# A hybrid attention, DeltaNet and ConvGLU layer: systems laid out in DRAM by DRAM to DRAM transfers, zeros stored at another place, and another distribution of late modulation

## The chip, the cores and the metric

The kernel runs on one core of a Trainium2 chip. The metric is the device time of one execution in microseconds. Three runs of the kernel before gave 1779.87, 1783.9 and 1786.72 us; their median is 1783.9 us. The core has a matrix engine (PE, with a separate weight load), three engines for elementwise work (DVE or VectorE, ACT or ScalarE, POOL or GpSimd) and SyncE (SP), which here only issues transfers. ACT issues some too. Sixteen DMA engines carry them.

## The reference, cut to what matters

The reference is one layer of a diffusion backbone, in float32, on 256 latent and 256 context tokens of width 2048. A normalised, modulated input goes through one wide projection; its columns feed latent attention (8 heads) and a gated DeltaNet (8 heads, two directions, chunks of 64 positions). Both branches are gated, added and projected; a gated MLP with a short convolution (ConvGLU) follows.

```python
shift1, scale1, gate1, shift2, scale2, gate2 = split(silu(c) @ w_ada + b_ada, 6)
p = modulate(rmsnorm(x, norm_mix), shift1, scale1) @ w_in    # and the same for ctx
# attention: 8 heads, latent queries over latent and context keys, one softmax
y_mla = softmax(q @ k.T / sqrt(192)) @ v
# DeltaNet, per head, direction and chunk of 64
m = where(strictly_lower, (beta * k) @ k.T * decay, 0)
u, w = triangular_solve(m + eye(64), [beta * v, beta * k * exp(gc)])
v_new = u - w @ s;  s = s * g_end + k_end.T @ v_new;  o = q @ s + A @ v_new
y_dn = rmsnorm(o) * silu(z)
x = x + gate1 * ((sig(g_a) * (y_mla @ w_o_mla) + sig(g_b) * (y_dn @ w_o_dn)) @ w_out)
x = x + gate2 * conv_glu(modulate(rmsnorm(x, norm_ffn), shift2, scale2))
```

The parts that the change touches are the 128 triangular systems of 64 x 64 (8 heads, 2 directions, 8 chunks) and the columns of `w_ada` that are needed late, for the second half of the layer.

## The kernel before

**Precision and the matrix work.** Every float32 product with a weight is split: ACT casts the weight to a high part (`whi`, L123), DVE computes the rest (`wlo`, L124), and PE multiplies with both (`mm_hl`, L156). Weights stream from DRAM in tiles of 512 KB (`raw`), issued by SP, with a ring of buffers. Each weight load waits until DVE and ACT have done with the buffer that it fills.

**Stages.** The first modulation and the first projections of all tokens come first (to about 145 us). Then the heads' stage builds, for each head, the inputs of the DeltaNet and the triangular matrices (to about 440 us). The attention follows in four pairs of heads (to about 722 us), then the scan of the DeltaNet, the output projections, and the ConvGLU (from about 1060 us, more than 700 us of matmuls).

**The systems.** The inverse of each 64 x 64 unit triangular matrix is built from 32 x 32 blocks. The two diagonal blocks of all 128 systems are read as one tile `ux` with 128 partitions and inverted on DVE by substitution (`inverse`, L822); `X[:, b]` is then the inverse of block b, one row of the tile for one system. `Xq` in DRAM takes it out of this form, once transposed (`xt`) and once as it stands; for groups of 16 systems q, `off_diagonal` (L855) reads it back as `xd` and multiplies it with the off-diagonal block `uo` on both sides, by PE with block diagonal tiles `bd`. All blocks end in the DRAM tensor `Tt`, which has for each direction and row of the 64 x 64 inverse 16 x 4 systems with 64 columns. The scan reads `Tt` from L1271 on (`tt<-Tt`, 721.7 us and later). The quarter of `Tt` below the diagonal is filled with zeros, by two transfers from the tile `none` (L656), issued by ACT at the start of the program.

**What sets the order.** Several generators are interleaved by hand: a `Side` runs its generator as far as a number of estimated nanoseconds that the main stream hands it. `fill` is the gate projections (L933), `inv` is `inverse` and then `off_diagonal`, `ada` the late modulation: 128 tiles of `wada2` (`rawa<-in_wada`, L262), each multiplied by a row and summed over its columns on DVE (1.2 us each). The attention's loop calls `side(c, r)` (L1179), which hands all three their share. PE's order is fixed where `pe.pinned` is set; `osync` and `odve` are the issuing engines with the place in the program kept, `sync`, `act` and `dve` can be shifted by the scheduler that lists each engine's instructions. `ada` must have reached fixed points before its sums are used, the last ones in the ConvGLU.

**Queues and counters.** Transfers issued by SP and by ACT signal their landing by eight counters, which the program uses in turn; an issuing engine works through its list in order, and a transfer that reuses a counter waits for the landing of the one before on it. In the listings below these counters are DMAHW0 to DMAHW7.

## Time and profile before

| What | Value |
| --- | --- |
| median of three runs | 1783.9 us (1779.87 to 1786.72) |
| the profiled execution's own time | 1786.89 us |
| its span (first to last instruction) | 1785.1 us |
| mean granted clock of PE | 0.985 |
| PE busy | 1737.5 us (97%) |
| DVE busy | 1356.8 us (76%) |
| ACT busy | 950.5 us (53%) |
| data moved by DMA | 417.15 MB in 190,260 packets, 56,912 of them under 512 B |

The profile is of one execution. Each row of a timeline gives the start in us, the duration, the engine, the line of the kernel, the operation and its tiles (output, arrow, input), and, in brackets, how long the engine stood idle before and what ended that. SPq and ACTq are the transfers' issues; an xN behind a row says that N like ones are put together, so the duration spans all of them with the pauses between. The table of windows has, for stretches of the span, the busy time and the number of instructions of each engine, the granted clock of PE (1.00 is full), the share of time in which the 16 DMA engines were busy, and the rate. The chain of waits follows the last instruction back to what released it.

The numbers of the stretches and of the waits are with the prediction.

### The profile page before, as it was taken

To read this page: it belongs to the slowest core of one execution; us is meant where nothing else is said; L and a number is where in the kernel's file an instruction comes from. 1 tells how busy PE (TensorE), PEld (TensorE's weight loads), DVE (VectorE), ACT (ScalarE), POOL (GpSimd) and SP (SyncE) were. 2 spreads that over 40 slices of the span, in tenths; PEclk is the share of its full clock that TensorE was granted. 3 is DMA by queue.
4 is the path that set the end of the run, shared out by engine and by line. 5 is a ranking of instruction groups with operands and counts; after the bars stand their busy time and mean duration, and the time that the engine had idled before them with its cause. 6 is when DMAs were issued, how large, how long until landed. Compare 5 with 4: busy or idle time off the path is not lost.

```text
span 1785.1 us, 34155 instructions
## 1 busy us (share of the span) xinstructions
PE 1737.5 (97%) x12957; PEld 1507.2 (84%) x12957; DVE 1356.8 (76%) x2696; ACT 950.5 (53%) x1966; POOL 41.4 (2%) x48
## 2 busy tenths in 40 slices
PE   7999999999799999999999999999999999999999
PEld 5887888888688888788878888888888888888888
DVE  4677799879578879787779979887788887655554
ACT  3335454454477766665646546555555555544443
POOL 0000011000000000000010000000000000000000
PEclk8999999999899999999989999999999999999999
DMA  9992588783578868999647968776667776666662
GB/s 348 407 373 93 150 235 249 230 257 109 138 255 248 260 214 273 360 339 361 233 130 233 328 199 281 232 237 207 202 219 229 228 225 201 182 198 199 198 199 87
DMA packets 190260, 417.15 MB, mean 234 GB/s; under 512 B 56912, under 2 KB 95696, under 8 KB 187792
## 3 DMA queue, kind: packets, MB, share of 16 engines
q1 hardware_dynamic: 165024, 401.59, 68.7%
q10 hardware_dynamic: 25072, 13.39, 2.5%
q8 instruction: 101, 1.65, 0.4%
q14 instruction: 63, 0.52, 0.1%
HBM read 387.00 MB, written 27.79 MB: 232 GB/s over the span
## 4 chain that ended last, share of the span: by engine, by line
PE 63%; issue 8%; DMA 1%; DVE 1%; ACT 0%; SPq 0%; POOL 0%; POOLq 0%; DVEq 0%
PE fps L68 27%; PE dps L68 13%; PE gtp L68 11%; PE brp L68 3%; PE vps L68 1%; PE kps L68 1%; PE qps L68 1%; PE sps L68 1%; PE kp L68 1%; PE ivp L68 1%; PE op L68 1%; PE yps L68 1%; PE yp L68 0%; DMA YM<-Ys 0%; SPq L851 0%
## 5 line engine op out<-in xcount | busy, mean ns | idle before, releaser
L123 ACT CAST whi<-raw 128x512 fp32r<-128x512 f32 (+1 forms) x940 | 578.9, 620 | 413.6 <-PE dps L68 113.5
L124 DVE TENSOR_TENSOR wlo<-raw,whi 128x512 fp32r<-128x512 f32 (+1 forms) x940 | 637.3, 686 | 211.4 <-ACT whi L123 203.5
L68 PE MATMUL fps<-H,whi 128*128 128x512 f32 x1376 | 475.0, 394 | 3.1 <-DVE H L1472 3.1
L68 PE MATMUL fps<-H,wlo 128*128 128x256 f32 x1376 | 372.3, 280 | 0.0
L68 PEld LDWEIGHTS fps<-H,whi 128*128 128x128 f32 x1376 | 253.7, 189 | 54.7 <-issue 1.9
L68 PEld LDWEIGHTS fps<-H,wlo 128*128 128x128 f32 x1376 | 259.7, 189 | 7.5 <-DVE wlo L124 0.5
L68 PE MATMUL gtp<-h,whi 128*128 128x512 f32 x640 | 231.4, 399 | 0.0
L68 PE MATMUL mmp<-h,whi 128*128 128x512 f32 x640 | 229.5, 400 | 0.0
L68 PE MATMUL dps<-GB,whi 128*128 128x512 f32 (+1 forms) x595 | 195.7, 377 | 0.0
L68 PE MATMUL mmp<-h,wlo 128*128 128x256 f32 x640 | 177.5, 283 | 0.0
L68 PE MATMUL gtp<-h,wlo 128*128 128x256 f32 x640 | 173.9, 282 | 0.0
L68 PE MATMUL dps<-GB,wlo 128*128 128x256 f32 x560 | 155.2, 282 | 0.0
L68 PEld LDWEIGHTS gtp<-h,whi 128*128 128x128 f32 x640 | 120.5, 190 | 25.3 <-issue 0.9
L68 PEld LDWEIGHTS mmp<-h,whi 128*128 128x128 f32 x640 | 119.8, 189 | 24.9 <-ACT dkx L531 0.3
L68 PEld LDWEIGHTS dps<-GB,whi 128*128 128x128 f32 x595 | 109.2, 188 | 20.2
L68 PEld LDWEIGHTS gtp<-h,wlo 128*128 128x128 f32 x640 | 121.5, 190 | 4.5
L68 PEld LDWEIGHTS mmp<-h,wlo 128*128 128x128 f32 x640 | 121.8, 190 | 3.6 <-issue 1.4
L68 PEld LDWEIGHTS dps<-GB,wlo 128*128 128x128 f32 x560 | 105.8, 189 | 0.6
L281 DVE CUSTOM_DVE_ANT_0 rawa<-rawa,sch 128x1024 f32<-128x1024 f32 x68 | 82.9, 1222 | 20.9 <-DMA rawa<-in_wada 19.4
L68 PE MATMUL fp<-h,gh 128*128 128x256 f32 (+1 forms) x448 | 85.5, 291 | 2.5 <-ACT h L68 1.7
L68 PEld LDWEIGHTS fp<-h,gh 128*128 128x128 f32 (+1 forms) x448 | 69.7, 190 | 7.6 <-issue 4.1
L68 DVE CUSTOM_DVE_ANT_0 rawa<-rawa,sch 128x1024 f32<-128x1024 f32 x60 | 72.9, 1218 | 0.0
(574 smaller groups left out, 2563.4 us busy)
## 6 DMA issues: line engine op xcount, KB each, us to landing
rawa<-in_wada SPq DMA_DIRECT2D x128, 512.0 KB, 5.2
raw<-in_wgate SPq DMA_DIRECT2D x82, 512.0 KB, 4.4
raw<-in_wval SPq DMA_DIRECT2D x82, 512.0 KB, 4.6
raw<-in_wdown SPq DMA_DIRECT2D x80, 512.0 KB, 4.2
wt<-in_wadas SPq DMA_DIRECT2D x16, 1024.0 KB, 9.6
raw<-in_wadab SPq DMA_DIRECT2D x32, 512.0 KB, 11.6
raw<-in_wgm SPq DMA_DIRECT2D x32, 512.0 KB, 5.6
raw<-in_wgd SPq DMA_DIRECT2D x32, 512.0 KB, 6.9
```

The lines of the kernel that those rows point to most:

```text
L68: i = f(*a, **k)
L123: act.copy(hi, raw)
L124: dve.tensor_tensor(out=lo, in0=raw, in1=hi, op=ALU.subtract)
L281: (odve if ada.bound else dve).tensor_tensor_reduce(out=w, in0=w, in1=sch, scale=1.0, scalar=0.0, op0=ALU.mult, op1=ALU.add, accum_out=par ...
```

## The change

It has five parts. (1) The two transfers of zeros to `Tt` are issued by SP, ahead of the heads' stage, and no longer by ACT at the start. (2) `inverse` stores three planes to `Xq` (the first block transposed, the first block, the second block), twelve transfers, and its sixteen stores `Tt<-ux` are gone. (3) A new function `place` copies blocks from DRAM to DRAM into `Tt`, for one q and one block in one transfer; `off_diagonal` calls it for the two diagonal blocks of each q, and for the off-diagonal one of the q before. (4) The off-diagonal block goes to a new DRAM tensor `Xo` by one transfer that ACT issues, where SP issued four to `Tt`. (5) `side` leaves `ada` out in the last four rounds of the attention's last pair and in the call behind it; those pieces of `ada` come later in the program.

```diff
--- before.py
+++ after.py
@@ -650,10 +650,9 @@
     Ud = dram.tile([4, 32, 2, 32, 32], F32, name="Ud")
     Uo = dram.tile([4, 32, 32, 32], F32, name="Uo")
 
-    Xq = dram.tile([2, 32, 4, 32, 32], F32, name="Xq")
+    Xq = dram.tile([3, 32, 4, 32, 32], F32, name="Xq")
+    Xo = dram.tile([32, 4, 32, 32], F32, name="Xo")
     Tt = dram.tile([P, 16, 4, 64], F32, name="Tt")
-    for d in range(2):
-        act.dma_start(Tt[64 * d + 32 : 64 * d + 64, :, :, 0:32].rearrange("c s g j -> c (s g) j"), none[:32].unsqueeze(1).broadcast_to([32, 64, 32]))
     As = dram.tile([4, P, 8, 64], F32, name="As")
     conv = mid.tile([P, 24, 3], F32, name="conv")
     dve.tensor_scalar(out=conv, in0=off["dn_conv"].rearrange("p (f w) -> p f w", w=3), scalar1=0.5, scalar2=None, op0=ALU.mult)
@@ -787,6 +786,8 @@
         gather(ps, P, xq[:, 0])
         return xs[0], xs[1], xq
 
+    for d in range(2):
+        osync.dma_start(Tt[64 * d + 32 : 64 * d + 64, :, :, 0:32].rearrange("c s g j -> c (s g) j"), none[:32].unsqueeze(1).broadcast_to([32, 64, 32]))
     ada = Side(ada_rest())
     ada.done, ada.bound = 0, True
     ins = {h: head_inputs(h) for h in (3, 0)}
@@ -842,13 +843,8 @@
         act.copy(xt, X[:, 0].rearrange("p c j -> p j c"))
         for g in range(4):
             gs = slice(32 * g, 32 * g + 32)
-            for n, x in enumerate((xt, X[:, 1])):
+            for n, x in enumerate((xt, X[:, 0], X[:, 1])):
                 sync.dma_start(Xq[n, :, g], x[gs])
-        for g in range(4):
-            for d in range(2):
-                for b in range(2):
-                    rs = slice(64 * d + 32 * b, 64 * d + 32 * b + 32)
-                    sync.dma_start(Tt[rs, :, g, 32 * b : 32 * b + 32].rearrange("c s j -> s c j"), X[32 * g + 16 * d : 32 * g + 16 * d + 16, b])
         yield 1000
         pI.close()
 
@@ -866,8 +862,13 @@
             sync.dma_start(uo, Uo[:, :, rs].rearrange("g j r i -> (g j) r i"))
             xd = pi.tile([P, 2, 4, 32], F32, tag="xd", name="xd", bufs=2)
             for n in range(2):
-                sync.dma_start(xd[:, n], Xq[n, rs].rearrange("r g j c -> (g j) r c"))
+                sync.dma_start(xd[:, n], Xq[2 * n, rs].rearrange("r g j c -> (g j) r c"))
             return uo, xd
+
+        def place(q, b, c, src):
+            rows = slice(64 * (q // 4) + 32 * b, 64 * (q // 4) + 32 * b + 32)
+            dst = Tt[rows, 4 * (q % 4) : 4 * (q % 4) + 4, :, 32 * c : 32 * c + 32]
+            sync.dma_start(dst.rearrange("c s g j -> (s g) c j"), src[4 * q : 4 * q + 4].rearrange("s g c j -> (s g) c j"))
 
         ahead = load(0)
         yield OD
@@ -875,6 +876,10 @@
             uo, xd = ahead
             if q < 7:
                 ahead = load(q + 1)
+            for n in range(2):
+                place(q, n, n, Xq[1 + n])
+            if q:
+                place(q - 1, 0, 1, Xo)
             for n in range(2):
                 src = uo if n == 0 else ip
                 for g in range(4):
@@ -887,10 +892,9 @@
                 if n == 0:
                     yield OC / 2
             act.copy(uo, ip)
-            for g in range(4):
-                dst = Tt[64 * (q // 4) : 64 * (q // 4) + 32, 4 * (q % 4) : 4 * (q % 4) + 4, g, 32:64]
-                sync.dma_start(dst, uo[32 * g : 32 * g + 32])
+            act.dma_start(Xo[4 * q : 4 * q + 4].rearrange("r g c i -> (g c) r i"), uo)
             yield OC / 2
+        place(7, 0, 1, Xo)
         pI.close()
 
     Ys = dram.tile([P, HEADS, T], F32, name="Ys")
@@ -1176,10 +1180,11 @@
     pairs = {}
     ryx = mid.tile([P, 2, T], F32, tag="krd", name="ryx")
 
-    def side(c, r):
+    def side(c, r, late=False):
         fill(r * c)
         inv(r * c)
-        ada(AD * c)
+        if not late:
+            ada(AD * c)
 
     pe.pinned = True
     for c in mla_project(0):
@@ -1206,10 +1211,10 @@
             for st in (pr, tail, at):
                 c = next(st, None)
                 if c is not None:
-                    side(c, R1 if b < 3 else 2.0)
+                    side(c, R1 if b < 3 else 2.0, b == 3 and n > 3)
             next(back, None)
         tail = at
-    side(2600, 1.0)
+    side(2600, 1.0, True)
     for _ in tail:
         pass
     inv.finish()
```

In the listings each engine's instructions stand in program order, with the counters or engines that an instruction waits for in brackets; names ending in q, s or a capital are tensors in DRAM or tiles as told above.

**SP at the start of the program** (`xl` and `xc` are the latent and the context tokens, `wt` the first weights). Before:

```order
L68 DMA xl<-in_xT 128x1024 [waits DMAHW0_49]
L68 DMA xc<-in_ctxT 128x1024 [waits DMAHW1_49]
L68 DMA xl<-in_xT 128x1024 [waits DMAHW2_49]
L68 DMA xc<-in_ctxT 128x1024 [waits DMAHW4_49]
L68 DMA wt<-in_wadas 128x2048 [waits DMAHW5_49]
L68 DMA wt<-in_wadas 128x2048 [waits DMAHW6_49]
```

and now:

```order
L68 DMA xl<-in_xT 128x1024
L68 DMA xc<-in_ctxT 128x1024 [waits DMAHW0_49]
L68 DMA xl<-in_xT 128x1024 [waits DMAHW1_49]
L68 DMA xc<-in_ctxT 128x1024 [waits DMAHW2_49]
L68 DMA wt<-in_wadas 128x2048 [waits DMAHW3_49]
L68 DMA wt<-in_wadas 128x2048 [waits DMAHW4_49]
```

The ninth load, the last `xc`, waited for the counter DMAHW4; it now waits for DMAHW2, and the others for counters one or two lower in the turn, since ACT's two transfers no longer take part here.

**SP at the end of the inverse** (`Xq`, `xd` and `Tt` as above; `raw<-in_wz` is the next weight of the gates). Before, behind the eight stores to `Xq` and fourteen of the sixteen to `Tt`:

```order
L851 DMA Tt<-ux 16x32x32 [waits DMAHW0_49]
L851 DMA Tt<-ux 16x32x32 [waits DMAHW1_49]
L869 DMA xd<-Xq 128x4x32 [waits DMAHW2_49]
L869 DMA xd<-Xq 128x4x32 [waits DMAHW3_49]
L869 DMA xd<-Xq 128x4x32 [waits DMAHW4_49]
L869 DMA xd<-Xq 128x4x32 [waits DMAHW5_49]
L129 DMA raw<-in_wz 128x1024 [waits DMAHW6_49,DVE_49]
L262 DMA rawa<-in_wada 128x1024 [waits DMAHW7_49,DVE_49]
L129 DMA raw<-in_wqb 128x1024 [waits DMAHW0_49,DVE_49]
```

and now, behind ten of the twelve stores to `Xq`:

```order
L847 DMA Xq<-ux 32x1024 [waits DMAHW4_49]
L847 DMA Xq<-ux 32x1024 [waits DMAHW5_49]
L865 DMA xd<-Xq 128x4x32 [waits DMAHW7_49,DMAHW6_49,DMAHW2_49]
L865 DMA xd<-Xq 128x4x32
L871 DMA Tt<-Xq 16x32x32 [waits DMAHW4_49,DMAHW0_49]
L865 DMA xd<-Xq 128x4x32 [waits DMAHW5_49,DMAHW1_49]
L865 DMA xd<-Xq 128x4x32
L871 DMA Tt<-Xq 16x32x32 [waits DMAHW3_49]
L129 DMA raw<-in_wz 128x1024 [waits DVE_49]
L262 DMA rawa<-in_wada 128x1024 [waits DVE_49]
```

The stores `Tt<-ux` are gone from ahead of the reads `xd<-Xq`; transfers `Tt<-Xq` stand between the reads, and the weights behind them. On DVE, the first instruction that makes use of the space that `ux` leaves is `km`, a key scale of the attention. Before:

```order
L124 TENSOR_TENSOR wlo<-raw,whi 128x512 [waits Activation_49]
L930 SCALAR_TENSOR_TENSOR zx<-zt,zx 128x256 [waits Activation_49]
L1035 SCALAR_TENSOR_TENSOR km<-ks,krm 128x4 [waits DMAHW4_49,DMAHW3_49,DMAHW5_49,DMAHW2_49,DMAHW6_49,DMAHW1_49,DMAHW7_49,DMAHW0_49,PE_49]
L124 TENSOR_TENSOR kt<-kps,kt 128x512 [waits Activation_49]
L1003 CAST rb_h<-km 128x4 [waits Pool_49]
```

and now:

```order
L124 TENSOR_TENSOR wlo<-raw,whi 128x512 [waits Activation_49]
L934 SCALAR_TENSOR_TENSOR zx<-zt,zx 128x256 [waits Activation_49]
L1039 SCALAR_TENSOR_TENSOR km<-ks,krm 128x4 [waits DMAHW4_49,DMAHW2_49,DMAHW5_49,DMAHW1_49,DMAHW6_49,DMAHW0_49,PE_49]
L124 TENSOR_TENSOR kt<-kps,kt 128x512 [waits Activation_49]
L1007 CAST rb_h<-km 128x4 [waits Pool_49]
```

It waited for all eight counters and now waits for six.

**ACT in the attention's last pair** (`s_` is a tile of scores: the exponential, then its normalisation; `ptp` and `PT` its transpose for PE; `YM` the attention's output, read back from `Ys` and split). Before:

```order
L1134 ACTIVATE s__8537,mns<-s__8537,mns,qm 128x512 [waits DVE_49]
L906 ACTIVATE zx<-zx 128x256 [waits DVE_49]
L123 CAST whi<-raw 128x512
L910 DMA Gs<-zx 128x256 [waits DMAHW3_49,Activation_49]
L1136 ACTIVATE s__8537<-s__8537,mns 128x512 [waits DVE_49]
L123 CAST PT<-ptp 128x4x128 [waits PE_49]
L123 CAST YM<-YM 128x2x256 [waits DMAHW1_49]
L123 CAST YM<-YM 128x2x256
```

and now:

```order
L1138 ACTIVATE s__8526,mns<-s__8526,mns,qm 128x512 [waits DVE_49]
L910 ACTIVATE zx<-zx 128x256 [waits DVE_49]
L123 CAST PT<-ptp 128x4x128 [waits PE_49]
L914 DMA Gs<-zx 128x256 [waits DMAHW7_49,Activation_49]
L123 CAST YM<-YM 128x2x256 [waits DMAHW5_49]
L1140 ACTIVATE s__8526<-s__8526,mns 128x512 [waits DVE_49]
L123 CAST YM<-YM 128x2x256
L123 CAST whi<-raw 128x512 [waits DMAHW1_49]
```

The first cast of `YM` stood behind the normalisation of the second tile of scores, and the transposes' cast `PT`; it now stands ahead of that normalisation.

## The prediction

> **What bounds the kernel now.** I read the page's first two parts, then the windows, then SP's timeline with the rows of PE, DVE and ACT beside it.
>
> ```profile
> span 1785.1 us, 34155 instructions
> PE 1737.5 (97%) x12957; PEld 1507.2 (84%) x12957; DVE 1356.8 (76%) x2696; ACT 950.5 (53%) x1966; POOL 41.4 (2%) x48
> ```
>
> PE is the bound: 1785.1 − 1737.5 = 47.6 us of idle time is all that waits can give back, beside the time lost to a reduced clock after them. PE's instructions and their order are the same in both kernels, so the change can only move waits. The windows show which resource is near its limit where the change works (columns: stretch, length, busy time and count of each engine, granted clock, DMA share, GB/s):
>
> ```profile
> 1.70:15.60 13.90, 10.15 (x72) 7.67 (x72) 7.24 (x15) 6.16 (x8) 0.20 (x2) 1.00 1.03 313
> 20.00:100.00 80.00, 74.01 (x840) 60.32 (x844) 50.16 (x75) 27.57 (x60) 1.02 (x1) 0.91 1.02 410
> 160.00:170.00 10.00, 10.00 (x39) 5.44 (x38) 7.76 (x13) 6.80 (x13) 0.00 (x0) 0.94 0.00 0
> 461.00:478.00 17.00, 11.21 (x87) 9.45 (x85) 4.22 (x7) 6.08 (x12) 0.00 (x0) 0.82 0.50 71
> 500.00:640.00 140.00, 140.00 (x1101) 123.48 (x1100) 115.14 (x250) 99.61 (x238) 7.80 (x7) 1.00 0.80 253
> ```
>
> Up to 100 us the DMA engines are full. At 160 to 170 us they are empty. At 461 to 478 us PE works 11.21 of 17 us at a clock of 0.82, with DMA half busy. From 500 to 640 us PE never stops, and a fifth of the DMA time is free.
>
> **The zeros.** In the timeline of the first microseconds (start, duration, engine, line, operation; in brackets the idle time before and what ended it):
>
> ```profile
> 1.67 0.67 ACTq L656 DMA_DIRECT2D Tt<-none  x1
> 5.57 0.33 SPq L68 DMA_DIRECT2D xl<-in_xT  x1
> 15.58 0.33 SPq L68 DMA_DIRECT2D xc<-in_ctxT  x1
> 20.30 0.69 DVE L68 TENSOR_TENSOR sq<-xc 128x512 f32<-128x512 f32 x1 [5.36 <-DMA xc<-in_ctxT]
> 21.14 1.81 PE L68 MATMUL pss<-sq,ones 128*32 128x512 f32 x8 [3.90 <-DVE sq L68]
> DMA to landing us min/median/max: 1.5/2.8/13.9
> ```
>
> The last row is that of the tile Tt. SP issues its eighth load at 5.57 and the ninth, the last part of the context, only at 15.58. In the order of before that ninth row waits for DMAHW4, one of eight completion counters that the loads and stores use in turn; 1.67 + 13.9 = 15.57, so it is the landing of the first store of zeros that it waits for. In the changed order the same row waits for DMAHW2, an early load. The eight loads of xl and xc are 4.2 MB, 10.2 us at 410 GB/s, so the last lands by about 13.4 instead of 20.3, and PE, which stood 3.90 us, finds it there. **Term: −3.9 us.** From below: 13.9 × (1 − 313/410) = 3.3 us is what the DMA engines lost in that stretch. From above: 20.3 − 13.4 = 6.9, where DVE and ACT would start that much sooner. The loads that keep the DMA engines full behind it start earlier too, so I expect the gain to be carried. The two stores cost the DMA engines about 4.6 us: the 3.3 and their own 0.5 MB, 1.3 us at 410 GB/s. In their new place these fall into the stretch of share 0.00, behind the load of 154.22 and ahead of that of 175.35, which by its row in the order waits for DVE anyway: nothing. With that cover gone it would be 4.6.
>
> ```profile
> 154.22 0.33 SPq L262 DMA_DIRECT2D rawa<-in_wada  x1
> 175.35 3.85 SPq L129 DMA_DIRECT2D raw<-in_wdv  x2
> ```
>
> **The end of the inverse.** The same views from 460 us:
>
> ```profile
> 457.45 0.41 SPq L846 DMA_DIRECT2D Xq<-ux  x1
> 457.90 0.42 SPq L846 DMA_DIRECT2D Xq<-xt  x1
> 460.33 17.87 SPq L851 DMA_DIRECT2D Tt<-ux  x16
> 478.24 2.53 SPq L869 DMA_DIRECT2D xd<-Xq  x4
> 480.88 0.45 SPq L129 DMA_DIRECT2D raw<-in_wz  x1
> 473.99 0.41 PE L68 MATMUL vps<-whi,kvn 128*128 128x256 f32 x1
> 480.91 0.60 PE L68 MATMUL ks<-ones,ksq 128*32 128x1 f32 x32 [6.51 <-DVE km L1035]
> 480.60 0.16 DVE L1035 SCALAR_TENSOR_TENSOR km<-ks,krm 128x4 f32<-128x4 f32 x1 [10.91 <-DMA xd<-Xq]
> 470.27 0.33 ACTq L910 DMA_DIRECT2D Zs<-zx  x1
> 485.75 0.62 ACT L123 CAST whi<-raw 128x512 fp32r<-128x512 f32 x1 [12.81 <-DMA raw<-in_wz]
> ```
>
> Sixteen stores of 512 pieces of 128 bytes hold SP for 17.87 us. The four xd reads and the next weights queue behind them. km on DVE waits for all eight counters in the order of before, thus for the last of these transfers; PE stands 6.51 us behind km. In the changed order km waits for six counters, which the twelve Xq stores use. The eight of before went out every 0.45 us or so (457.45, 457.90) and ended at 460.3; four more end near 462 and, with the 2.5 us that the xd transfers of the same counters took, land near 464.5, before PE's matmul at 473.99 ends. So the 6.51 us go. The clock too: PE runs slowly behind the wait.
>
> ```profile
> 484.81 0.63 PE L68 MATMUL gtp<-h,whi 128*128 128x512 f32 x1
> 485.24 0.41 PE L68 MATMUL gtp<-h,wlo 128*128 128x256 f32 x1
> 485.45 0.44 PE L68 MATMUL gtp<-h,whi 128*128 128x512 f32 x1
> 487.23 0.39 PE L68 MATMUL gtp<-h,whi 128*128 128x512 f32 x1
> 487.58 0.39 PE L68 MATMUL gtp<-h,whi 128*128 128x512 f32 x1
> 471.29 0.43 PE L68 MATMUL ks<-ones,ksq 128*32 128x1 f32 x32 [2.19 <-ACT ksq L1024]
> ```
>
> One pair takes 0.64 us up to 485.45 (484.81 to 485.45) and 0.35 later (487.23 to 487.58). Over 480.91 to 485.45 that is 4.54 × (1 − 0.35/0.64) = 2.1 us lost. The earlier wait, 2.19 us at 471.29, stays, and its slow stretch, now cut off at 474.4, would run on to about 475.8 if it is as long: 0.6 lost anew. Net 1.4. **Term: −6.5 − 1.4 = −7.9 us.** What is late next: the second of the new transfers to Tt waits for the counter of the Zs store (issued 470.27; the row below, of the chain of waits, has its 1.87 us to landing), so raw<-in_wz leaves SP near 472.3 instead of 480.88, and whi near 477 instead of 485.75. The gtp matmuls of the second row below, the first with that weight, began at 492.02, 11 us behind the wait, hence near 484 in the changed kernel: no new wait. From below, 6.5 − 2.5 = 4.0, if km still ended on reads like xd's; from above 6.5 + 2.1 = 8.6.
>
> ```profile
> 470.27 1.87 DMA Zs<-zx
> 492.02 2.79 PE gtp L68 x16
> ```
>
> **The transfers in the attention.** Added to 480 to 640 us: 16 transfers Tt<-Xq and 8 Tt<-Xo of 512 pieces each, 12,288 pieces read and written in DRAM; the 8 Xo stores replace the 32 Tt<-uo stores piece for piece. SP issues 3 transfers for each system where it issued 4, so its queue is no longer; ACT issues one, 0.33 us by Zs' row, in a stretch where it is busy 99.61 of 140 us. No row shows a DRAM to DRAM transfer. From below, the 128-byte stores of 461 to 478: 0.50 × 17 × 16 / 8192 = 17 ns a piece. From above, a read and a write apart, 34 ns. Added DMA time: 12,288 × 17/16 = 13 us or 26 us, to 28 us that are free (0.20 × 140). At 17 ns the share becomes 0.89, at 34 ns 0.99. The store is the nearest row, since the copy writes the same pieces to the same tensor, so I take 17, nothing lost; from above, the stretch with share 1.02 kept PE at 74.01 of 80 us, 7.5%, which over 140 us is +10 us. [...]
>
> **The last pair.**
>
> ```profile
> 698.60 0.38 SPq L1191 DMA_DIRECT2D YM<-Ys  x1
> 704.52 0.60 PE L68 MATMUL ptp<-ident,s__8537 128*128 128x128 f32 x4
> 705.73 1.15 ACT L123 CAST YM<-YM 128x512 fp32r<-128x512 f32 x2 [1.08 <-DMA YM<-Ys]
> 717.83 1.22 DVE L68 CUSTOM_DVE_ANT_0 rawa<-rawa,sch 128x1024 f32<-128x1024 f32 x1
> 719.72 1.86 PE L68 MATMUL yps<-PT,V 128*128 128x512 f32 x8 [3.52 <-DVE PT L124]
> ```
>
> About three modulation products (1.22 us of DVE each) and their loads go to the feed-forward stage. The product at 717.83 stands right ahead of the PT that PE awaits for 3.52 us; without it PE gains 1.2, or up to 2.2 if earlier ones go too. But in the changed ACT order the cast of YM stands ahead of the second softmax's normalisation. YM lands at 705.7, cast 0.6 and normalisation 0.7 follow, so PE's transpose of 704.52 starts near 706.9: +2.4, which then also makes the later stall shorter. **Term: 0**, between −1.5 and +2.5. [...]
>
> **Sum.** −3.9 − 7.9 + 0 + 0 = −11.8. The profiled execution took 1786.9 us (span 1785.1 and 1.8 around it), 3.0 above the median of 1783.9. So 1775.1 for an execution like it, and **1772 us** against the median.
>
> **Rivals.**
> 1. *The copies fill the DMA engines.* They decide from 28 × 16 / 12,288 = 36 ns a piece, where the free time is used up; beyond, each ns costs 0.77 us, and weights reach PE late in the attention. At 52 ns the gain is gone, at 72 ns it is 27.6 − 11.8 = +16: 1800. For it: the share of 0.80 is a mean, and nothing shows the copy's price. Against: it would need four times the store's.
> 2. *The start gains nothing.* The loads behind are bound by DMA, and PE could meet its next wait 3.9 us later. 1783.9 − 7.9 = 1776. For it: a share of 1.02 to 100 us. Against: those loads start earlier as well.
> 3. *The last pair loses.* The 2.4 us stay and a slow stretch of 2.1 follows: 1772 + 4.5 = 1776.5. For it: ACT's order. Against: DVE has less to do at the stall behind.
> 4. *The last pair gains.* YM lands sooner beside other loads, ACT isn't late at the second ptp, and the 3.5 us at yps go whole: 1768.5. For it: three products of 1.22 us leave a stretch in which DVE has no idle time. Against: ACT's order, as in rival 3.
>
> **How the numbers follow.** Half a per cent, 8.9 us, is about what a measurement of this kernel can tell from no change: faster means below 1775.0, slower above 1792.8. Chances: the forecast 0.58, rival 1 0.10, rival 2 0.15, rival 3 0.10, rival 4 0.07. Of the forecast's 0.58, 0.06 lie above 1775 (its own range is 1766 to 1777: −7.3 with both lower bounds, −15.5 with both upper ones, and 2.5 for the last pair, of which not all comes together). Rivals 2 and 3 lie 1 to 1.5 us above the bound: 0.15 same, 0.10 faster. Rival 1: 0.08 slower, 0.02 same. Faster 0.52 + 0.10 + 0.07 = 0.69, same 0.23, slower 0.08. The range: below, rival 4 with the start's upper bound, 1768.5 − 3.0 and the runs' scatter of 3: 1763. Above, the forecast with +10 for a share near 1.0: 1782.
>
> **What would show it.** Right: the last xc issued by 6 us and PE's wait before pss gone; km without a DMA wait near 474, raw<-in_wz issued near 472, the clock's dip there once; 500 to 640 us at PE 140.00 with a DMA share near 0.9; PE's wait at yps below 2 us, one at the second ptp. Wrong: landings of Tt<-Xq far above 3 us with a share of 1.0 and PE idle in the attention (rival 1); main stages that start less than 3 us sooner (rival 2); a second slow stretch near 705 us (rival 3).

## The result, and the profile after

The changed kernel takes 1834.1 us in the median (1831.6 to 1841.3) against 1784.0 for the kernel before on the same chip (1779.9 to 1786.7): a ratio of 1.029 with an interval of 1.0252 to 1.0327. It is 50 us slower; the forecast was 1772, 12 us faster.

The page of the kernel after, its span and the busy time of each engine:

```profile
span 1829.9 us, 34114 instructions
PE 1755.0 (96%) x12957; PEld 1514.3 (83%) x12957; DVE 1357.7 (74%) x2696; ACT 947.3 (52%) x1966; POOL 41.7 (2%) x48
```

PE runs the same 12957 matmuls and was busy for 17.5 us longer (1737.5 before), and it stood still for 74.9 us instead of 47.6. To see where, the start of the same PE instruction was taken from both traces, all along the program (after minus before):

| place (time in the kernel before) | after − before, us | change in the stage, us |
|---|---|---|
| start, 60 us | −4.2 | −4.2 |
| ahead of the end of the inverse, 420 us | −8.2 | −4.0 |
| start of the attention, 500 us | −15.1 | −6.9 |
| end of its main part, 640 us | +35.4 | **+50.5** |
| behind the last pair, 740 us | +37.9 | +2.5 |
| end of the scan, 880 us | +45.8 | **+7.9** |
| from 1081 us to the end | +44.8 | −1.0 |

Two of the change's parts did what was foreseen. In the timeline of the kernel after (start, duration, engine, line, operation; in brackets the idle time before and what ended it), the start of the program and the new place of the zeros:

```profile
15.59 0.69 DVE L68 TENSOR_TENSOR sq<-xc 128x512 f32<-128x512 f32 x1 [1.33 <-DMA xc<-in_ctxT]
17.19 1.19 PE L68 MATMUL pss<-sq,ones 128*32 128x512 f32 x8
149.44 3.55 SPq L68 DMA_DIRECT2D Tt<-none  x2
...
465.56 0.43 PE L68 MATMUL ks<-ones,ksq 128*32 128x1 f32 x32 [2.19 <-ACT ksq L1028]
466.07 0.16 DVE L1039 SCALAR_TENSOR_TENSOR km<-ks,krm 128x4 f32<-128x4 f32 x1 [2.10 <-PE ks L68]
467.56 0.43 PE L68 MATMUL ks<-ones,ksq 128*32 128x1 f32 x32
```

PE's `pss` starts at 17.19 instead of 21.14, with no wait. `km` waits for PE and for no transfer any more, and the `ks` behind it, for which PE had stood 6.51 us, starts without a wait at 467.56 instead of 480.91.

Everything is lost behind that. The windows of the kernel after (stretch, length, busy time and count of PE, PEld, DVE, ACT, POOL, granted clock, DMA share, GB/s), first the stretch that the prediction showed of before, then the whole of the attention's main part:

```profile
500.00:640.00 140.00, 114.53 (x819) 95.77 (x818) 82.58 (x180) 73.96 (x176) 6.96 (x6) 0.90 0.61 194
485.10:675.60 190.50, 157.53 (x1100) 132.09 (x1099) 119.19 (x251) 100.99 (x238) 8.07 (x7) 0.91 0.60 191
```

and the same main part in the windows of the kernel before:

```profile
500.20:640.10 139.90, 139.90 (x1099) 123.40 (x1098) 115.04 (x250) 99.50 (x238) 7.80 (x7) 1.00 0.80 253
```

What took 139.90 us without a gap takes 190.50: 33.0 us (190.50 − 157.53) PE stands, and 17.6 us (157.53 − 139.90) it works longer, at a clock of 0.91. The DMA engines are not full; their share *fell* from 0.80 to 0.60. So the wait isn't for a transfer that is slow but for one that is issued late. The timeline of the kernel after shows who issues late, here around one of these stops (the SP rows are all that SP issued from 497 to 519 us):

```profile
497.74 0.33 SPq L129 DMA_DIRECT2D raw<-in_wz  x1
498.12 1.33 SPq L871 DMA_DIRECT2D Tt<-Xq  x2
514.55 0.93 SPq L865 DMA_DIRECT2D xd<-Xq  x2
517.12 0.33 SPq L862 DMA_DIRECT2D uo<-Uo  x1
517.49 0.52 SPq L871 DMA_DIRECT2D Tt<-Xo  x1
518.13 0.55 SPq L129 DMA_DIRECT2D raw<-in_wz  x1
...
513.55 0.97 PE L68 MATMUL ivp<-xd,bd 128*128 128x32 f32 x8
524.08 1.14 ACT L123 CAST whi<-raw 128x512 fp32r<-128x512 f32 x2 [0.40 <-ACT zx L935]
524.75 0.51 PE L68 MATMUL gtp<-h,whi 128*128 128x512 f32 x1 [3.38 <-ACT whi L123]
```

SP issues nothing from 499.45 to 514.55. What it stands at is the read `xd<-Xq`, which fills a buffer that PE's `ivp` matmuls have to give back: PE ends them at 514.5 (513.55 + 0.97), and SP goes on at 514.55. No weight leaves SP from 498.07 to 518.13. The weight of 518.13 is in its buffer, cast and at PE 6.6 us later (524.75), and PE has by then stood 3.38 us. Of the 6.6 us, 4.8 are the landing; ACT, whose list has rows `zx` of a gate ahead of the cast, starts it 1.1 us after that. At three other stops of PE, at 494.77, 552.63 and 604.04 (5.47, 3.30 and 5.23 us), the cast starts within 0.02 us of the landing, so there only the late issue counts. The same gap of SP comes back group by group, at 478.6 to 489.3, 527.6 to 542.1, 560 to 570.8 and 579.9 to 593 (this last one at a store `Ys<-ryx` of the attention's output). In the order of the changed kernel this piece of SP's list reads (line, operation, what it waits for):

```
L871 DMA Tt<-Xq 16x32x32 [waits DMAHW5_49]
L871 DMA Tt<-Xq 16x32x32 [waits DMAHW6_49]
L865 DMA xd<-Xq 128x4x32 [waits DMAHW0_49,PE_49]
L865 DMA xd<-Xq 128x4x32 [waits DMAHW1_49]
L862 DMA uo<-Uo 128x128 [waits DMAHW7_49,DMAHW2_49,Activation_49]
L871 DMA Tt<-Xo 16x32x32 [waits DMAHW3_49]
L129 DMA raw<-in_wz 128x1024 [waits DMAHW4_49,DVE_49]
```

The reads wait for PE in the kernel before too, and there too a weight stands behind them. What differs is how far ahead of its use the weight stands. For each weight behind such a wait I counted, in the orders, PE's instructions between the matmul for which SP waits and the first matmul that uses the weight. One PE instruction takes 0.127 us here (139.90 / 1099), so the 6.6 us from issue to use are some 52 of them, and the 10.2 us from the end of `ivp` (514.52), with the rows that SP issues ahead of the weight, some 80. In the kernel before the shortest of these leads are 83, 91, 91, 95: the wait is hidden. In the kernel after they are 2, 18, 26, 34, 43, 43, 50: all too short.

The last pair and the scan, in the timeline and the windows of the kernel after:

```profile
741.85 0.62 ACT L123 CAST YM<-YM 128x512 fp32r<-128x512 f32 x1 [3.20 <-DMA YM<-Ys]
743.15 0.66 PE L68 MATMUL ptp<-ident,s__8526 128*128 128x128 f32 x4 [2.99 <-ACT s__8526 L1140]
757.66 2.68 PE L68 MATMUL yps<-PT,V 128*128 128x512 f32 x8 [1.87 <-DVE PT L124]
```

```profile
743.00:745.00 2.00, 1.85 (x9) 1.61 (x10) 1.64 (x5) 2.00 (x6) 0.00 (x0) 0.83 1.00 368
745.00:747.00 2.00, 2.00 (x7) 1.61 (x7) 2.00 (x6) 2.00 (x5) 0.00 (x0) 0.50 0.48 191
747.00:749.00 2.00, 2.00 (x11) 1.79 (x10) 1.83 (x5) 1.61 (x5) 0.00 (x0) 0.82 0.84 219
749.00:752.00 3.00, 3.00 (x20) 2.65 (x19) 2.70 (x6) 2.92 (x7) 0.00 (x0) 1.00 0.79 234
```

ACT waits 3.20 us for `YM` ahead of the second normalisation, so PE stands 2.99 us at the second `ptp`, and its clock is down for the next 6 us; the wait of 3.52 us at `yps` shrinks to 1.87 us in return. And the scan, which the change only touches by what is left for it, is 8 us longer. The tile views give both stretches as one row each (number of instructions, shortest, median and longest in ns, first and last start), of before:

```profile
L68 PE MATMUL ivp<-xd,bd x128: 190/276/276, 494.6 to 630.9; 128*128 128x32 f32 x128
L1273 SPq DMA_DIRECT2D tt<-Tt x8: 319/326/510, 721.7 to 845.1; - x8
```

and of after:

```profile
L68 PE MATMUL ivp<-xd,bd x128: 190/276/401, 479.5 to 665.9; 128*128 128x32 f32 x128
L1278 SPq DMA_DIRECT2D tt<-Tt x8: 320/382/628, 758.4 to 890.9; - x8
```

From the first to the last `ivp` it takes 136.3 us before and 186.4 after; from the first to the last read of `Tt` in the scan 123.4 and 132.5. These two lengths are the gauge of the experiments.

### The profile page after: what moved, and what is told of

It is laid out like the page before. It is cut to its first block, busy times and chain, and to the rows that moved or that the text cites. A ratio compares the mean times of both kernels' runs of the same rounds, so it can differ in the third digit from the quotient of the medians.

```text
span 1829.9 us, 34114 instructions
## 1 busy us (share of the span) xinstructions
PE 1755.0 (96%) x12957; PEld 1514.3 (83%) x12957; DVE 1357.7 (74%) x2696; ACT 947.3 (52%) x1966; POOL 41.7 (2%) x48
## 3 DMA queue, kind: packets, MB, share of 16 engines
q8 instruction: 101, 1.65, 0.4%
## 4 chain that ended last, share of the span: by engine, by line
PE 58%; issue 8%; DMA 3%; DVE 3%; ACT 2%; POOL 0%; SPq 0%; ACTq 0%; POOLq 0%; DVEq 0%
PE fps L68 26%; PE dps L68 13%; PE gtp L68 9%; PE brp L68 2%; DMA raw<-in_wgm 2%; PE vps L68 1%; PE kps L68 1%; DMA rawa<-in_wada 1%; DVE wlo L124 1%; PE qps L68 1%; PE ivp L68 1%; ACT whi L123 1%; PE sps L68 1%; PE kp L68 1%; DVE rawa L68 1%
## 5 line engine op out<-in xcount | busy, mean ns | idle before, releaser
L68 PE MATMUL gtp<-h,whi 128*128 128x512 f32 x640 | 240.3, 410 | 21.5 <-ACT whi L123 21.5
L68 PE MATMUL gtp<-h,wlo 128*128 128x256 f32 x640 | 179.0, 290 | 1.8 <-DVE wlo L124 1.8
L68 PEld LDWEIGHTS gtp<-h,whi 128*128 128x128 f32 x640 | 124.9, 196 | 49.7 <-ACT whi L123 23.7
L68 PEld LDWEIGHTS gtp<-h,wlo 128*128 128x128 f32 x640 | 125.6, 196 | 10.0 <-DVE wlo L124 5.4
```

What stands on the lines that cost most here:

```text
L68: i = f(*a, **k)
```

## The experiments

Three theories. **S**, the place in the list: rows that wait for PE stand on SP ahead of weights that PE needs soon. **D**, the copies themselves: 12,288 pieces read and written in DRAM are dear, or hold what others wait for. **L**, the late modulation: work left for the scan costs there what was saved before.

### The parts that should gain, without the copies

The kernel before with the zeros moved (e7_zeros), and with that and the late modulation (e4_zeros_late).

```diff
-    for d in range(2):
-        act.dma_start(Tt[64 * d + 32 : 64 * d + 64, :, :, 0:32]...
...
+    for d in range(2):
+        osync.dma_start(Tt[64 * d + 32 : 64 * d + 64, :, :, 0:32]...
     ada = Side(ada_rest())
...  # e4_zeros_late alone:
-        ada(AD * c)
+        if not late:
+            ada(AD * c)
```

> The kernel before with the zeros stored by SP ahead of the heads' stage, alone. The run with zeros and late modulation gained 8.9 us up to 480 us and gave them back in the last pair and the scan. If the late modulation's edit did that, 1775 to 1778 us; if the zeros' place itself does (for example the loads of the scan come in another phase), 1786 us as before.

> The kernel before with two parts of the change alone: the zeros stored by SP ahead of the heads' stage, and no late modulation in the last four rounds of the last pair. Inverse and copies as before. From the comparison of the two traces: the start gains 6.7 us up to 180 us, the last pair and the scan lose 2.5 + 7.9 if the late modulation is their cause. Theory S and D: no loss from 500 to 640 us; 1784 - 6.7 = 1777 us without the late modulation's loss, 1787 us with it.

The zeros alone: 1782.4 us against 1786.9, ratio 0.9976 (0.9958 to 0.9994), 4.4 us gained. With the late modulation: 1788.0 against 1786.1, ratio 1.0019 (0.9999 to 1.0038). The attention takes 136 us in both (487.3 to 623.6 and 485.9 to 622.1), so none of the 50 us are here. But the scan's reads of `Tt` take 125.7 us in e7 and 130.2 in e4: L is real, some 7.7 us by the two ratios (0.0043 × 1784), and is not the main loss.

### Moving what waits, on SP

e1_loadend takes the next group's reads to the end of the group; e2_bufs3 gives `uo` and `xd` a third buffer, so that the reads wait for an earlier PE group; e3_double is e1 with each copy made a second time into a DRAM tensor that nothing reads, to price a copy.

```diff
 e1:        uo, xd = ahead
-            if q < 7:
-                ahead = load(q + 1)
...
             act.dma_start(Xo[4 * q : 4 * q + 4]...
+            if q < 7:
+                ahead = load(q + 1)
 e2:
-            xd = pi.tile([P, 2, 4, 32], F32, tag="xd", name="xd", bufs=2)
+            xd = pi.tile([P, 2, 4, 32], F32, tag="xd", name="xd", bufs=3)
 e3, in place(), beside e1:
+            dst = Tu[rows, 4 * (q % 4) : 4 * (q % 4) + 4, :, 32 * c : 32 * c + 32]
+            sync.dma_start(dst.rearrange("c s g j -> (s g) c j"), src[4 * q : 4 * q + 4]...
```

> The changed kernel with one edit: off_diagonal asks for the next group's uo and xd at the end of its iteration, not at its start. All 24 copies within DRAM stay. In SP's list the reads xd<-Xq, which wait for PE's product ivp, then stand behind more of the weights. Theory S (SP's list: the weights that PE needs next are queued behind a read that waits for PE itself): the 50.6 us lost between 500 and 640 us go, and the time is 1775 to 1787 us. Theory D (the copies of 128-byte pieces within DRAM are dear, or hold the counters): they are all still there, so the time stays within 10 us of 1834. Theory L (late modulation moved out of the last pair): no effect on these 50 us.

> The changed kernel with a third buffer for uo and xd, all else as it is. The read xd<-Xq of a group then waits for the product of one group earlier, long done when SP comes to it. Theory S: the 50.6 us go, 1775 to 1787 us. Theory D: within 10 us of 1834, since the copies are the same.

> The kernel of the first run (reads at the end of the iteration) with each of the 24 copies within DRAM made twice, the second time into a DRAM tensor that nothing reads. Theory S: the copies are cheap while they block nothing, so within 5 us of the first run. Theory D: if 24 copies cost 50 us, 24 more cost about 50 again, 1825 us or more. The share of the DMA engines between 500 and 640 us gives the price of a piece: 12,288 more pieces at 17 ns are 13 us of DMA, at 34 ns 26 us.

1832.3 us (ratio 1.0262, 1.024 to 1.0284), 1830.4 (1.0247, 1.0221 to 1.0272) and 1849.1 (1.0347, 1.033 to 1.0365). Neither e1 nor e2 cured anything: `ivp` takes 190.2 and 182.7 us. SP's timeline tells why, of e1:

```profile
503.11 1.85 SPq L871 DMA_DIRECT2D Tt<-Xq  x2
516.82 0.51 SPq L871 DMA_DIRECT2D Tt<-Xo  x1
```

and of e2, with ACT's rows:

```profile
501.99 2.13 SPq L871 DMA_DIRECT2D Tt<-Xq  x2
516.61 0.51 SPq L871 DMA_DIRECT2D Tt<-Xo  x1
517.22 0.56 SPq L129 DMA_DIRECT2D raw<-in_wz  x1
...
514.47 0.27 ACT L894 COPY uo<-ivp 128x128 f32<-128x128 f32 x1 [1.13 <-PE ivp L68]
514.76 0.38 ACTq L895 DMA_DIRECT2D Xo<-uo  x1
```

SP now stands at the next row of the same kind: the copy `Tt<-Xo` waits for ACT's store `Xo`, which waits for PE's `ivp`, and the weight stands behind the copy. My expectation of S, that freeing the reads would free the weights, missed: there are two such rows in each group, and one is enough. e3 fits neither theory's figure (+17 us to e1), and its own list is worse, with leads of 2, 10, 15, 18. So it gives no price of a copy. Over the kernel before and those in which SP issues the copies one by one, a short lead and a long stretch go together, if not in strict order (the kernel after has a shorter lead than e1, and the shorter stretch of the two):

| kernel | shortest leads, PE instructions | first to last `ivp`, us |
|---|---|---|
| before | 83, 91, 91, 95 | 136.3 |
| e2_bufs3 | 26, 34, 43 | 182.7 |
| after | 2, 18, 26, 34 | 186.4 |
| e1_loadend | 18, 26, 34 | 190.2 |
| e3_double | 2, 10, 15, 18 | 201.0 |

### The copies from another engine

The same 24 copies, with the same bytes, issued by ACT (e5_allact), by ACT without the late modulation (e6_allact_nolate), 16 of them by ACT and 8 by SP (e8_qact), by POOL (e9_allpool), and by POOL without the late modulation (e10_allpool_nolate). If D were right, the loss would stay with any issuer.

```diff
 in place():
-            sync.dma_start(dst.rearrange("c s g j -> (s g) c j"), src[4 * q : 4 * q + 4]...
+            act.dma_start(dst.rearrange("c s g j -> (s g) c j"), src[4 * q : 4 * q + 4]...   # e5, e6; e8: Xq's alone
+            pool.dma_start(dst.rearrange("c s g j -> (s g) c j"), src[4 * q : 4 * q + 4]...  # e9, e10
 e6 and e10:
-                    side(c, R1 if b < 3 else 2.0, b == 3 and n > 3)
+                    side(c, R1 if b < 3 else 2.0)
...
-    side(2600, 1.0, True)
+    side(2600, 1.0)
```

> The changed kernel with one edit: ACT issues the 24 copies within DRAM, SP none. The copies, their bytes and their waits are the same, but in SP's list no weight stands behind a copy. The first two experiments left the loss where it was, and in their traces SP stood before the copy Tt<-Xo (12.5 us up to 516.61 in the second), which waits for ACT's store Xo and so for PE's second product ivp: theory S is kept in a wider form (any row of SP's list that waits for PE, xd<-Xq or Tt<-Xo, ahead of weights that PE needs soon). By the lists, the weight with the shortest way is used 2, 18 and 26 PE instructions behind the PE instruction that its issue depends on in the changed kernel, 83 or more in the kernel before, 72 or more here. Theory S: the 50 us from 500 to 640 us go, 1775 to 1787 us. Theory D (the copies themselves are dear, or hold counters that loads wait for): 1825 us or more. If ACT's own waits at the copies matter, something between.

> As the run before, and the late modulation in the last pair as in the kernel before. If the late modulation's edit costs what the zeros' run suggests (about 2 us at the last pair, about 8 in the scan), this is 8 to 10 us below the run before. Theory S: 1766 to 1778 us, below the kernel before by 6 to 18.

> The changed kernel with the 16 copies Tt<-Xq issued by ACT and the 8 copies Tt<-Xo by SP as in the change. The shortest way between a weight's last dependence on PE and its use is 55 PE instructions, then 71. Theory S: nearly all of the 50 us go, a few us stay where the way is 55 (some 7 us of PE time, against 5 us landing and 1.3 us for cast and difference): 1778 to 1792 us. Theory D: 1825 or more.

> The changed kernel with one edit: GpSimd (POOL), which is busy 2% of the span, issues the 24 copies within DRAM. They are the same copies, but stand in a list of their own and signal eight counters of their own; the lists of SP and ACT hold no wait for them, and the shortest way from a weight's last dependence on PE to its use is 83 PE instructions, as in the kernel before. Issued by ACT they left 30 of 50 us. Theory S (the loss is the engines that stand behind a copy, first SP, then ACT): the whole 50 us go, and with the late modulation's loss of some 9 us still in, 1775 to 1787 us. Theory D (the copies are dear for the DMA engines): 1810 us or more, as with ACT.

> As the run before, with the late modulation of the last pair as in the kernel before. Theory S: the start's gain and that of the inverse's end stay and nothing is lost: 1765 to 1776 us, 10 to 20 below the kernel before. Theory D: 1800 us or more.

| kernel | median, us | ratio to before | first to last `ivp`, us |
|---|---|---|---|
| e5_allact | 1815.0 | 1.0150 (1.0122 to 1.0177) | 168.2 |
| e6_allact_nolate | 1804.0 | 1.0098 (1.0078 to 1.0118) | 168.4 |
| e8_qact | 1803.0 | 1.0081 (1.0054 to 1.0108) | 153.7 |
| e9_allpool | 1794.5 | 1.0054 (1.0038 to 1.0069) | 145.6 |
| e10_allpool_nolate | 1782.2 | 0.9988 (0.9971 to 1.0005) | 148.9 |

The loss depends on who issues the copies, with the same copies: 50 us in the attention on SP, 32 on ACT, 9 to 13 on POOL (`ivp` against 136.3). That speaks for S and against D. It isn't zero elsewhere, and a part of that is shown: the copies then stand ahead of that engine's own work. In the timeline of ACT in e5:

```profile
504.83 0.52 ACTq L871 DMA_DIRECT2D Tt<-Xo  x1
505.39 0.83 ACT L1107 CAST qt<-qx 64x256 fp32r<-64x256 f32 x2 [6.28 <-DMA Xo<-uo]
```

ACT stands 6.28 us at a copy until the store `Xo` has landed, and its casts of weights and queries with it. That is the one long wait of this kind in e5, some 6 of ACT's 32 us; the rest shows in e12. On POOL, in the waits of e10 from 482 to 720 us (engine, line, for what; total, times, longest):

```profile
POOL Tt L871 <- issue: 43.6, 12, 7.1
DVE qm L1116 <- POOL qm L175: 11.9, 4, 9.2
```

DVE waits up to 9.2 us for a power of 128x4 numbers that POOL computes (`qm`), which it waited 0.9 us for at most before. That these waits, 11.9 us in all, are POOL's 9 to 13 us is likely, not shown. POOL gets out one copy of 512 pieces in about 4 us: three in a row start at 499.11, 502.92 and 506.91. Leaving the late modulation out gains 9.3 us on ACT and 11.8 on POOL by the ratios (1.0150 to 1.0098, 1.0054 to 0.9988).

e11_allpool_double is e10 with each copy made twice, as in e3; e12_bufs3_xo2_allact is e5 with three buffers and `Tt<-Xo` two groups later, so that it waits for a store that has long landed.

```diff
 e12:
-            if q:
-                place(q - 1, 0, 1, Xo)
+            if q > 1:
+                place(q - 2, 0, 1, Xo)
```

> As the run before, with each copy made twice, the second time into a DRAM tensor that nothing reads. Theory S: within 4 us of the run before, with a DMA share that is higher by 0.06 to 0.1 from 500 to 640 us (12,288 pieces at 13 to 17 ns over 16 engines are 10 to 13 us). Theory D: slower by as much again as the copies cost.

> The copies issued by ACT as in the fifth run (1815 us), but with a third buffer for uo and xd, and Tt<-Xo two groups behind its store Xo instead of one, so that neither ACT nor SP comes to a transfer whose source is still under way. Theory S: what was left of the loss with ACT (some 30 us) is ACT and SP standing at such transfers, so most of it goes: 1780 to 1795 us. If it is ACT's time for issuing 24 copies, or the waits for counters, it stays at 1805 us or more.

e11 took 1806.9 us (ratio 1.0129, 1.0099 to 1.0159), 25 us more than e10, where S gave almost nothing (the 13 ns a piece in its expectation is an estimate that no row shows). Its waits show POOL's time to issue (137.0 us ahead of its copies, 43.6 in e10, with no wait that the profile shows), not the DMA engines (share 0.71 from 480 to 660 us): the wait of `qm` for POOL grew from 11.9 to 36.9 us in all. So doubling on POOL prices POOL, and again not the copy. e12 took 1818.1 us (1.0188, 1.0151 to 1.0225) and `ivp` 166.7 us, no better than e5; its expectation missed. Up to 650 us no copy holds ACT for more than about 0.4 us in e12, so ACT's 30 us are not spent standing at copies. What they are shows at a stop of PE, in the timelines of SP, ACT and PE in e12:

```profile
544.57 0.33 SPq L129 DMA_DIRECT2D raw<-in_wqb  x1
...
560.19 0.37 ACT L519 COPY zx<-gtp 128x256 f32<-128x256 f32 x1 [1.04 <-PE gtp L68]
...
562.80 2.70 ACT L123 CAST whi<-raw 128x512 fp32r<-128x512 f32 x5
563.47 0.50 PE L68 MATMUL qps<-qan__4753,whi 128*128 128x512 f32 x1 [3.32 <-ACT whi L123]
```

The weight landed 4.5 us after its issue, at 549.1, and lay in its buffer for 13.7 us. ACT's list has its cast behind `zx<-gtp`, which waits for the gate product that PE ends right ahead of `qps`, and behind more rows of the gate and of the systems. So the order of ACT's list came out badly too, whoever waits at the copies. The lead can be counted for a cast as well, from the last PE instruction that its place in ACT's list depends on: the shortest are 38 in the kernel before, 39 in e9 and 37 in e13 (below), but 1 in the kernel after, in e5, e8 and e12, although SP's shortest lead in e12 is 69.

### The same pieces in six copies

e13_lump_nolate issues the same 12,288 pieces from SP, in six copies of 2048 instead of 24 of 512: one for each direction and block of `Tt`, each in a group by which its source has long been stored, and without the late modulation. e14_lump is e13 with the late modulation, thus the changed kernel in all but this.

```diff
-        def place(q, b, c, src):
...
+        def place(d, b, c, src):
+            rows = slice(64 * d + 32 * b, 64 * d + 32 * b + 32)
+            dst = Tt[rows, :, :, 32 * c : 32 * c + 32]
+            sync.dma_start(dst.rearrange("c s g j -> (s g) c j"), src[16 * d : 16 * d + 16]...
...
-            for n in range(2):
-                place(q, n, n, Xq[1 + n])
-            if q:
-                place(q - 1, 0, 1, Xo)
+            if q in (1, 2, 3, 4):
+                place((q - 1) // 2, (q - 1) % 2, (q - 1) % 2, Xq[1 + (q - 1) % 2])
+            if q == 5:
+                place(0, 0, 1, Xo)
...
-        place(7, 0, 1, Xo)
+        yield OC
+        yield OC
+        place(1, 0, 1, Xo)
```

> The changed kernel with the late modulation as before, and the same 12,288 pieces copied within DRAM by SP in six transfers of 2048 pieces (one for each direction and block) in place of 24 of 512; the copies of Xo come one for each direction, after all its stores. By the lists the shortest way from PE to a weight's use is 83 PE instructions, as in the kernel before (2, 18, 26 in the changed one). Theory S (place in SP's list): no loss from 500 to 640 us, the gains of the start (4 to 7) and of the inverse's end (7 to 8) stay: 1768 to 1778 us. Theory D (price of the copies, landing, counters): the pieces are the same and a landing is longer, so 1800 us or more.

> As the run before, but without late modulation in the last four rounds of the last pair, as in the change. If that edit costs by itself what it cost with the copies on ACT and on POOL (11 and 12 us): 9 to 13 us above the run before. If its cost came from their lists: within 4 us.

e13 took 1774.0 us (1771.5 to 1776.7) against 1784.7, ratio 0.9942 (0.9922 to 0.9961): faster than both kernels. e14 took 1782.6 against the same, ratio 0.9989 (0.9975 to 1.0003). The windows and the tile views of e13:

```profile
500.00:640.00 140.00, 140.00 (x1107) 123.12 (x1107) 111.11 (x245) 97.60 (x228) 7.95 (x7) 1.00 0.84 263
```

```profile
L871 SPq DMA_DIRECT2D Tt<-Xq x4: 517/535/557, 468.6 to 528.5; - x4
DMA to landing us min/median/max: 4.4/6.5/9.0
L68 PE MATMUL ivp<-xd,bd x128: 190/276/276, 480.4 to 616.6; 128*128 128x32 f32 x128
L1280 SPq DMA_DIRECT2D tt<-Tt x8: 319/326/432, 707.7 to 832.3; - x8
```

With all the copies made, PE never stops from 500 to 640 us; `ivp` takes 136.2 us, the shortest leads are 83 and 91 again, and the DMA share is 0.84. That settles D: the pieces cost the DMA engines something and PE nothing, although they land late (4.4 to 9.0 us after the issue, in the row above, which spans all transfers of `Tt`). It confirms S in a wider form, the place of loads and casts in the lists, with two reservations. e13 has fewer rows on SP and other places at once; that 24 copies aren't too many by their number follows from e9 and e10, where they left SP and most of the loss went. And the leads of SP and of ACT's casts are both long in e9 and e13 and both short in the kernel after, so no run tells how its 50 us divide between the two lists; e5 and e12, with SP's leads long and ACT's short, lose 30 to 32.

e14 against e13 is the late modulation alone: 8.4 us by the ratios. Its attention is as good (136.3 us for `ivp`); the scan isn't. The reads of `Tt` take 129.1 us instead of 124.6, and in the waits from 800 to 880 us stand, of e14:

```profile
ACT gk L912 <- DVE gk L520: 20.4, 5, 6.7
DVE rawa L281 <- DMA rawa<-in_wada: 13.8, 5, 4.0
DVE rawa L281 <- DMA sch<-Sc: 6.6, 1, 6.6
PE kp L68 <- DVE S L1356: 2.6, 2, 2.5
```

and of e13:

```profile
DVE rawa L281 <- DMA rawa<-in_wada: 6.6, 4, 2.4
ACT gk L912 <- DVE gk L520: 6.4, 4, 2.3
```

DVE stands at modulation products whose loads haven't landed, 20.4 us against 6.6, and the gate `gk`, the scan's state `S` and, at the end, PE's `kp` wait behind it. The scan has as many products in both (22 or 23); each just stands elsewhere, ahead of its load. It is again a row in one engine's list that holds what is behind it.

## Why the prediction was wrong, and where it was right

**The start** (−3.9): right. −4.0 at `pss`, −4.2 at 60 us, and 4.4 by the medians of e7 alone. The gain was carried, so rival 2 is refuted. Between 60 and 420 us the two traces part by 4.0 us more, which was not foreseen. Most of it is clock: the granted clock from 155 to 185 us is 1.00 where it was 0.94, behind a wait at `cps` of 0.51 us where it was 1.53 (2.5 us together), and 1.00 where it was 0.91 from 400 to 420 us (1.5 us). The trace of e7 shows the same 4.0 us. Whether the two slow stretches belong to the kernel before or to its one profiled execution, which lies 3.0 us above its median, is open.

**The inverse's end** (−7.9): right in place and cause. −6.9 in the kernel after, although a slow clock (0.83 from 440 to 460 us, where it was 1.00) took 2.5 us back just ahead of it. The 2.19 us wait at `ksq` stayed, as foreseen; the slow stretch behind it didn't come in the kernel after (last section).

**The copies in the attention** (0): wrong by 50.6 us, and the only term that matters. The step that failed is the sentence that SP "issues 3 transfers for each system where it issued 4, so its queue is no longer", with "nothing lost" behind it. It counted the rows of the list; what counts is which of them wait for PE and how far ahead of its use the weight behind them stands. The order of the changed kernel shows both, without any time: the lead falls from 83 PE instructions to 2. It also took ACT's part to be one issue of 0.33 us, and in ACT's list the shortest lead of a cast fell from 38 to 1. The prediction read the orders at the start, at the inverse's end and in the last pair, where a wait of before would go, and not in the stage where PE never waited. SP's empty 15.1 us (499.45 to 514.55) show what has to be weighed: the read that waited for `ivp` held every row behind it in SP's list, until 0.03 us after PE had ended `ivp` at 514.52.

Rival 1 had the sign and the symptom (weights late in the attention) but by another mechanism: full DMA engines, at 36 ns a piece and more. The share was 0.61 in its stretch, and 0.84 in e13 with PE busy throughout, so the price of a piece, whether 17 ns or another, stays far from where it would decide: the same 128-byte pieces cost PE nothing in e13 (busy for 140.00 of 140.00 us).

**The last pair** (0, −1.5 to +2.5): right for the pair, at its upper end. The wait at the second `ptp` came (2.99 us; 2.4 foreseen), the clock went down behind these 2.99 us as in rival 3 (0.83, 0.50 and 0.82 over 6 us, 1.7 us of work), and the wait at `yps` fell by 1.65 us, to 1.87: +2.5 net.

**What was not priced:** the products that the last pair no longer does don't only go to the feed-forward stage; the order of those in the scan changes, and that cost 7.9 us in the kernel after and 8 to 12 us by the ratios in four pairs of kernels.

The sum without the last pair's edit, −11.8 us, is near what e13 measured: 1784.7 − 1774.0 = 10.7. The gains were there; the order that SP's and ACT's lists got with the 24 copies and the order of the modulation took 50 and 8 us.

**Open:** why the scheduler put the reads and copies, and ACT's rows that wait for PE, so much earlier against PE's work when the copies are many and small (the leads are read from its lists, not explained); the price of a copy by itself, which neither doubling gave; and how the 50 us divide between SP's list and ACT's.

## What to carry to other kernels

SP issued its transfers in the order of its list here, and the read that waited for PE held the weights behind it: none left SP from 498.07 to 518.13 us. So count for each weight behind such a row how much of PE's work lies between the wait and the use, and compare it with the time from the end of the wait to the use (10.2 us here, 6.6 of them from the weight's issue), before counting rows or bytes. Count the same for the casts behind the rows that wait for PE in another engine's list: in e12 a weight lay landed for 13.7 us. When a stage gets slower and the DMA share falls (0.80 to 0.60 here), look for the engine that issues late, not for a slow transfer; and another issuer can have work of its own behind the transfers (ACT stood 6.28 us at one copy in e5). Here fewer, larger copies with sources that are long finished cost PE nothing (140.00 of 140.00 us busy in e13), where the lists made with many small ones cost 50 us.

## What the hardware showed that was not expected

The clock behind the same wait of 2.19 us at `ksq` differs. In the windows of after and, below, of e13:

```profile
465.00:470.00 5.00, 4.43 (x91) 4.22 (x92) 3.29 (x9) 2.78 (x6) 1.28 (x2) 1.00 0.36 63
```

```profile
465.00:470.00 5.00, 4.76 (x84) 4.50 (x85) 3.63 (x9) 2.63 (x6) 1.01 (x1) 0.66 0.62 171
```

The granted clock is 1.00 in one and 0.66 in the other, with a wait of 2.19 us at 465.56 and 465.24. So the length of that one wait doesn't decide it alone. What else does is not shown. And a copy within DRAM of 512 pieces, whose issue takes about 0.5 us on SP (0.52 for `Tt<-Xo` in the kernel after) and ACT (0.52 in e5), came on POOL only about 4 us after the one before: 0.63 us of its own, and 3.18 and 3.36 us ahead of those at 502.92 and 506.91 in e10 with no wait that the profile shows.
